# A hybrid decoder layer on one Trainium2 core: u and y of the state-space layer re-laid through DRAM instead of by TensorE transposes, with a new spread of the filler products and a new split of the first feed-forward products

## The chip, the core and the metric

The kernel runs on one core of one Trainium2 chip. The metric is the device time of one execution in microseconds (us); the time of a kernel is the median of its runs.

## The reference

One layer of a decoder with 1024 tokens and a model width of 1024, all in float32. Three token mixers read column blocks of one projection of the normed input, their outputs are gated and summed, and a SwiGLU feed-forward follows:

```
h = rms_norm(x, mix_norm_g)
(u, c_b, c_c, c_x, q, k_c, v_c, ..., nsa_gates, mix_gates) = split(h @ w_in)
y_ssm  = s5_mixer(u, ...)                          # 32 groups of 16 channels, 64 complex states each
y_conv = short_conv_mixer(c_x, c_b, c_c, ...)      # width-3 causal convolution, 512 channels
y_attn = nsa_mixer(q, ...)                         # compressed, selected and window attention, 8 heads
x = x + (g0 * y_ssm + g1 * y_conv + g2 * y_attn) @ w_out
h = rms_norm(x, ffn_norm_g)
x = x + (silu(h @ w_gate) * (h @ w_up)) @ w_down   # hidden width 2816
```

In `s5_mixer` a state runs along the tokens, `s[t] = lam_bar * s[t-1] + b_bar u[t]`; `y = Re(c s) + d * u` goes through GELU, then through a gated linear unit (`ssm_w_glu`).

## The kernel before

**Dense products.** Every large product is made of two-part numbers: `split` writes a rounded high part with ScalarE (L61) and the remainder with VectorE (L62), and `prod` issues three matmuls of 128x512 per 128 rows of depth (L120, L122, L124). Weights come as pages of 128x1024 in the order of `weight_list`. `weights()` hands out the next page; when it does, it splits that page and `LOOK` pages ahead, and issues the loads of `AHEAD` pages beyond the last split one. `LOOK` is 1 and `AHEAD` 2 in the stages spoken of here. Working tiles of 128x1024 share 44 buffers ("pages"), tiles of 128x512 share 14; PSUM is divided into four tiles of 128x512 (`acc`) and two of 128x1024 (`wide`).

**Order.** The program is traced once, and a planner makes the order of each engine from it at build time, by the place in the program and by when it reckons the operands to be ready. Each engine and the DMA queue of SyncE (SP) then works in that fixed order. `k.filler` is a generator of dense products; `fill(n)` draws n matmuls from it at that place of the program. In the state-space stage the filler is `tail`: the convolution mixer (12 blocks of 48 matmuls) and the two plain gated projections `mix_plain` (8 pages of 48 matmuls), 960 matmuls in all. `drain` draws the rest.

**The state-space stage.** `u_rows` computes u token-major (tokens on partitions), writes it to DRAM and reads it back with eight interleaved token sets beside each other (`UN`, 32 DMAs at L702). Tokens are handled in 128 chunks of 8; channels in 4 quarters q of 8 groups. For each quarter `s5` does:

- `s5_kernel`: the 8-token kernel of a group (16 matmuls L969), spread by 16 DMAs into `M` (L980);
- `s5_order` and `s5_tokens`: ScalarE reorders `UN` into `UG` (L1001), TensorE transposes it (8 matmuls against the identity, L1010), ScalarE copies the result to `UT` (L1011);
- `s5_carry`, `s5_inputs`: `cp` by 4 DMAs (L958), `Bm` by 8 transposes (L991);
- `s5_scan`: 16 matmuls (L1021), then VectorE multiplies and scans along the chunks (L1037 to L1060), with `beat()`, which is `fill(F5B)`, behind each operation; then the tables of the next quarter (L895, L930 to L947), again a beat behind each operation;
- `s5_out`: y of a chunk from `U` and `M` (L1071) and from the carried state `X` and `cp` (L1075), GELU on ScalarE (L1078), 8 transposes (L1084), a ScalarE copy to `yT` (L1085), and the split into parts (`mhi`, `mlo`).

`mix_ssm` then reads the parts of all four quarters, quarter by quarter in each sum.

**Around the feed-forward's start.** `out_rows` ends with the row norms of the last four token tiles; their normed rows `xn` are transposed (L1361) into operands `B` of a Strassen-like product. The generator `ffn_up` is advanced between those steps with `next(up)`: it issues products of 12 matmuls (L1505) until its next `yield`. The yields stand in front of products 3, 6, 9 and 12 (counted from 0).

Of the kernel before, what the change touches and what calls it, by code (L numbers as in the profile page):

```python
# [8 lines left out]
F32 = mybir.dt.float32  # L9
F32R = mybir.dt.float32r  # L10
# [5 lines left out]
P = 128  # L16
# [17 lines left out]
class Trunk:  # L34
# [639 lines left out]
                yield from self.block(w, (self.hh, self.hl), range(KD), evac)  # L674


    def u_rows(self):
        nc = self.nc
        W = [self.weights() for _ in range(4)]
        self.UN = [self.page("UN") for _ in range(4)]  # L680
        self.tab = {}

        def ahead():
            yield from self.s5_phases()
            yield from self.s5_tables(0, self.tab)
        steps = ahead()
        spill = self.dram.tile([S, HALF], F32, tag="su", name="su")
        for t in range(NT):
            ps = self.acc()
            tok = slice(t * P, (t + 1) * P)  # L690
            yield from self.prod(ps, (lambda k: self.hh[k][:, tok], lambda k: self.hl[k][:, tok]),
                                 (lambda k: W[k // 2][0][:, (k % 2) * 512:(k % 2) * 512 + 512],
                                  lambda k: W[k // 2][1][:, (k % 2) * 512:(k % 2) * 512 + 512]), range(KD))
            u = self.half("u")
            nc.scalar.activation(u, ps, AF.Copy)
            nc.sync.dma_start(spill[tok], u)
            for _ in range(8):
                next(steps, None)
        chunk = spill.rearrange("(n j) c -> j n c", j=8)
        for q in range(4):  # L700
            for k in range(8):
                nc.sync.dma_start(self.UN[q][:, k * P:(k + 1) * P], chunk[7 - k][:, q * P:(q + 1) * P])  # L702
        self.run(steps)


    def conv_rows(self):
        nc = self.nc
        self.cv, self.gp, self.gn_at = [], {}, 0
        for c in range(4):
            if c == 3:  # L710
                self.gate_fetch(0)
                self.gate_fetch(1)
            cb, cy, cv = self.page("cb"), self.page("cy"), self.page("cv")
            z = self.page("z")

            def evac_c(half, s, ps):
                nc.scalar.activation(cb[:, s], ps, AF.Copy)

            def evac_x(half, s, ps):
                nc.vector.tensor_tensor(z[:, s], ps, cb[:, s], op=OP.mult)  # L720
                if half == 0:
                    return
                w = [self.par[:, R_CW + k * 4 + c:R_CW + k * 4 + c + 1] for k in range(3)]
                nc.vector.tensor_scalar(cy, z, w[2], None, op0=OP.mult)
                nc.vector.scalar_tensor_tensor(cy[:, 1:], z[:, :1023], w[1], cy[:, 1:], op0=OP.mult, op1=OP.add)
                nc.vector.scalar_tensor_tensor(cy[:, 2:], z[:, :1022], w[0], cy[:, 2:], op0=OP.mult, op1=OP.add)

            def evac_b(half, s, ps):
                nc.vector.tensor_tensor(cv[:, s], ps, cy[:, s], op=OP.mult)
            for evac in (evac_c, evac_x, evac_b):  # L730
                yield from self.block(self.weights(), (self.hh, self.hl), range(KD), evac)
            self.cv.append(self.halves(cv))


    def cmul(self, eng, o, a, b, t, conj=False):
# [259 lines left out]
        self.fill(2 * self.F5)  # L995
        return B

    def s5_order(self, q):

        self.ug[q] = self.page("UG")  # L1000
        self.nc.scalar.activation(self.ug[q].rearrange("p (g k h) -> p g k h", g=8, k=8),  # L1001
                                  self.UN[q].rearrange("p (k g h) -> p g k h", k=8, g=8), AF.Copy)

    def s5_tokens(self, q):
        nc = self.nc
        U = self.page("UT").rearrange("p (g n) -> p g n", g=8)
        un = self.ug.pop(q)
        ps = self.wide()
        for g in range(8):
            nc.tensor.transpose(ps[:, g * P:(g + 1) * P], un[:, g * P:(g + 1) * P], self.ident)  # L1010
        nc.scalar.activation(U.rearrange("p g n -> p (g n)"), ps, AF.Copy)  # L1011
        self.fill(2 * self.F5)
        return U

    def s5_scan(self, q, U, B, ep):
        nc = self.nc
        v = nc.vector
# [44 lines left out]
        return X  # L1062

    def s5_out(self, q, U, M, X, cp):
        nc = self.nc
        Y = self.page("YN").rearrange("p (t g h) -> p t g h", t=8, g=8)
        ps = self.wide()
        for half in range(2):
            b = ps[:, half * 512:half * 512 + 512]
            for j in range(4):  # L1070
                nc.tensor.matmul(b[:, j * P:(j + 1) * P], U[:, half * 4 + j], M[:, half * 2 + j // 2, j % 2],  # L1071
                                 start=j == 0, stop=False, skip_group_check=True)
            for j in range(4):
                a, g = half * 2 + j // 2, j % 2
                nc.tensor.matmul(b[:, j * P:(j + 1) * P], X[:, a, g], cp[:, a, g], start=False, stop=j == 3,  # L1075
                                 skip_group_check=True)
            self.fill(self.F5)
        nc.scalar.activation(Y.rearrange("p t g h -> p g t h"), ps.rearrange("p (g t h) -> p g t h", g=8, t=8),  # L1078
                             AF.Gelu_apprx_tanh)
        self.fill(self.F5)  # L1080
        yT = self.page("yT")
        ps = self.wide()
        for t in range(8):
            nc.tensor.transpose(ps[:, t * P:(t + 1) * P], Y[:, t].rearrange("p g h -> p (g h)"), self.ident)  # L1084
        nc.scalar.activation(yT.rearrange("p (n t) -> p t n", t=8), ps.rearrange("p (t n) -> p t n", t=8), AF.Copy)  # L1085
        self.fill(self.F5)
        self.yT.append(self.halves(yT))

    F5, F5S = 8, 16
    F5B = 3  # L1090

    def beat(self):

        self.fill(self.F5B)

    def s5(self):
        self.yT, self.ug = [], {}
        tab = self.tab
        for q in range(4):
            bp, cr, bb, ep = tab.pop(q)  # L1100
            M = self.s5_kernel(q, cr, bb)
            if q == 0:
                self.s5_order(0)
            cp = self.s5_carry(cr)
            U = self.s5_tokens(q)
            B = self.s5_inputs(q, bp)
            if q < 3:
                self.s5_order(q + 1)
            self.F5B = 3 if q < 3 else 5
            X = self.s5_scan(q, U, B, ep)  # L1110
            if q < 3:
                for _ in self.s5_tables(q + 1, tab):
                    self.beat()
            self.fill(self.F5S)
            self.s5_out(q, U, M, X, cp)


    def halves(self, x):
# [274 lines left out]
    def ffn_up(self):  # L1393
# [84 lines left out]
            operand(n)  # L1478
        yield
        for n, (i, z, p) in enumerate(flat):  # L1480
            if n in (3, 6, 9, 12):
                yield
            if n == len(flat) - 5:
                self.down = self.ffn_down()
# [145 lines left out]
    def weight_list(self):  # L1630
        i = self.i
        w = i["w_in"][0]
        ks = [self.cols(w, 4 * a, 4, C_KS, 256) for a in range(2)]
        kw = [self.cols(w, 3 * b, min(3, KD - 3 * b), C_KW, 280) for b in range(3)]
        L = [ks[0], kw[0], ks[1], kw[1], kw[2]]
        L += [self.cols(w, 0, KD, C_KC, P), self.cols(w, 0, KD, C_VC, P)]
        L += [self.cols(w, 2 * a, 2, C_Q, 512) for a in range(4)]
        w1 = [self.cols(i["cmp_w1"][0, n // 4], 4 * (n % 4), 4, 0, 256, "w1") for n in range(8)]
        g = [self.cols(w, 0, KD, C_MG + n * P, P, "g") for n in range(24)]
        L += g[:2] + w1[:3] + g[2:3] + w1[3:7] + g[3:4] + w1[7:] + g[4:]  # L1640
        L += [self.cols(w, 2 * a, 2, C_U, 512) for a in range(4)]
        for c in range(4):
            L += [self.cols(w, 0, KD, c0 + c * P, P) for c0 in (C_C, C_X, C_B)]
        for m in (i["conv_w_out"][0], i["nsa_w_o"][0]):
            L += [self.cols(m, 0, 4, d * 256, 256) for d in range(4)]
        gl = i["ssm_w_glu"][0]

        def glu(d):
            def f(t):
                v = t.rearrange("p (z k c) -> p z k c", z=2, k=4)  # L1650
                return [(v[:, z], gl[:, z * D + d * P:z * D + d * P + P].rearrange("(k p) c -> p k c", p=P))
                        for z in range(2)]
            f.used, f.key = 1024, None
            return f
        L += [glu(d) for d in range(KD)]
        return L
# [3 lines left out]
def trunk_kernel(ctx, tc, ins, out):  # L1660
# [61 lines left out]
        k.fill(n or 1)  # L1722
    k.attention()
    k.drain()
    k.run(k.u_rows())

    def tail():
        yield from k.conv_rows()
# [7 lines left out]
                o.append(k.halves(raw[d - 4]))  # L1736
        yield from k.mix_plain(1, k.cv, True, split)
        yield from k.mix_plain(2, o, False)
    k.filler = tail()
    k.fill(24)  # L1740
    k.s5()
    k.drain()
    k.run(k.mix_ssm())
    k.out_rows()
    k.run(k.down)
# [23 lines left out]
```

## Time and profile before

| what | value |
|---|---|
| median of 3 runs (lowest to highest) | 1762.75 us (1761.01 to 1764.09) |
| the profiled execution: its time, its span | 1763.58 us, 1761.7 us |
| mean granted TensorE clock over the span | 0.999 |
| TensorE matmul busy | 1738.1 us (99% of the span), 8701 matmuls |
| VectorE, ScalarE, GpSimd busy | 1198.2 us (68%), 793.7 us (45%), 83.7 us (5%) |
| DMA queue of SyncE | 184.08 MB, 32.5% of the 16 engines' time |

The span is the time from the first to the last instruction of the profiled execution; 1.9 us of that execution lie outside it. TensorE's busy time counts a matmul from its start to its modelled end, which overlaps the next one, so the engine's rate is read from the starts of successive matmuls.

### The profile page before, as it was taken

The numbers are of one execution on the slowest core, as the hardware profiler recorded it, in microseconds if no ns is written. First come the engines' busy times: TensorE is split into PE (matmuls) and PEld (weight loads), VectorE is DVE, ScalarE is ACT, GpSimd is POOL, SyncE is SP. The second block draws the span as 40 slices with busy tenths as digits, with TensorE's granted clock in tenths as the row PEclk, the third lists the DMA queues.
The fourth block names the chain that finished last, engine by engine and source line by source line (L and its number), as shares of the span: only waits on it lengthen the run. The fifth ranks groups of instructions, "written<-read, shape, count | busy, mean of one in ns | idle before, by whom it ended". The sixth has DMA issues, their size and how long they took to land.

```text
span 1761.7 us, 23773 instructions
## 1 busy us (share of the span) xinstructions
PE 1738.1 (99%) x8701; PEld 1440.4 (82%) x8701; DVE 1198.2 (68%) x2434; ACT 793.7 (45%) x1469; POOL 83.7 (5%) x86
## 2 busy tenths in 40 slices
PE   8999999999999999999999999999999999999999
PEld 7987788888888888888888888778888888888887
DVE  6975456666666670856875687698667776697681
ACT  6415567777777842222132234742223233344360
POOL 0000000000000000000000000002112111110000
PEclk9999999999999999999999999999999999999999
DMA  5213422221211123322554323433222322477521
GB/s 171 73 43 103 122 84 67 60 61 45 60 41 49 55 83 91 83 60 73 179 175 137 108 96 102 144 120 127 101 96 102 120 96 90 169 272 252 163 95 48
DMA packets 166202, 185.60 MB, mean 105 GB/s; under 512 B 17642, under 2 KB 122182, under 8 KB 166086
## 3 DMA queue, kind: packets, MB, share of 16 engines
q1 hardware_dynamic: 166053, 184.08, 32.5%
q8 instruction: 69, 1.13, 0.3%
q14 instruction: 48, 0.39, 0.1%
q10 hardware_dynamic: 32, 0.01, 0.0%
HBM read 132.40 MB, written 45.35 MB: 101 GB/s over the span
## 4 chain that ended last, share of the span: by engine, by line
PE 82%; DVE 9%; ACT 4%; issue 2%; SPq 1%; DMA 1%; DVEq 0%; ACTq 0%; POOL 0%
PE wide L1505 12%; PE acc L124 11%; PE acc L120 11%; PE acc L122 11%; PE acc L1612 7%; PE acc L1505 7%; PE wide L1612 5%; PE acc L560 3%; PE wide L519 3%; PE acc L1274 2%; PE wide L1274 2%; DVE A L62 2%; PE acc L582 2%; PE acc L583 2%; PE wide L257 1%
## 5 line engine op out<-in xcount | busy, mean ns | idle before, releaser
L1505 PE MATMUL wide<-B,A 128*128 128x512 f32 x1056 | 250.8, 391 | 0.6 <-ACT A L61 0.3
L120 PE MATMUL acc<-hh,whi 128*128 128x512 f32 x608 | 243.4, 400 | 2.8 <-DVE kl L66 1.5
L124 PE MATMUL acc<-hh,wlo 128*128 128x512 f32 x608 | 243.0, 400 | 1.4 <-DVE wlo L62 1.4
L122 PE MATMUL acc<-hl,whi 128*128 128x512 f32 x608 | 243.1, 400 | 0.0
L1505 PEld LDWEIGHTS wide<-B,A 128*128 128x128 f32 x1056 | 196.6, 188 | 47.5 <-DVE sg L1518 3.3
L1505 PE MATMUL acc<-B,A 128*128 128x512 f32 x792 | 192.1, 393 | 0.5 <-ACT p L1508 0.5
L1505 PEld LDWEIGHTS acc<-B,A 128*128 128x128 f32 x792 | 149.2, 189 | 32.6 <-ACT p L1508 1.6
L62 DVE TENSOR_TENSOR wlo<-raw,whi 128x1024 fp32r<-128x1024 f32 (+1 forms) x75 | 90.6, 1211 | 72.4 <-ACT whi L61 56.0
L120 PEld LDWEIGHTS acc<-hh,whi 128*128 128x128 f32 x608 | 114.6, 188 | 21.0 <-issue 2.0
L124 PEld LDWEIGHTS acc<-hh,wlo 128*128 128x128 f32 x608 | 114.8, 189 | 18.8 <-DVE wlo L62 2.1
L61 ACT ACTIVATE A<-S 128x512 fp32r<-128x512 f32 x88 | 55.0, 627 | 166.8 <-DVE S L1437 166.0
L122 PEld LDWEIGHTS acc<-hl,whi 128*128 128x128 f32 x608 | 114.6, 189 | 17.3 <-issue 0.2
L62 DVE TENSOR_TENSOR ptl<-acc,pth 128x512 fp32r<-128x512 f32 (+1 forms) x152 | 93.8, 619 | 48.6 <-ACT pth L61 47.4
L1612 PE MATMUL acc<-wdp,act 128*128 128x512 f32 x528 | 121.2, 389 | 0.0
L524 DVE CUSTOM_DVE_ANT_0 p<-wide,mask 128x640 f32<-128x640 f32 (+7 forms) x128 | 90.1, 705 | 43.2 <-PE wide L519 40.5
L1612 PEld LDWEIGHTS acc<-wdp,act 128*128 128x128 f32 x528 | 99.1, 188 | 20.6
L527 ACT ACTIVATE p<-p,small 128x640 f32<-128x640 f32 (+7 forms) x128 | 93.6, 732 | 37.0 <-DVE small L524 34.9
L61 ACT ACTIVATE pth<-acc 128x512 fp32r<-128x512 f32 (+1 forms) x152 | 80.9, 534 | 45.2 <-PE acc L560 44.4
L61 ACT ACTIVATE whi<-raw 128x1024 fp32r<-128x1024 f32 (+1 forms) x75 | 77.6, 1045 | 52.2 <-DVE m L1154 15.9
L120 PE MATMUL acc<-mhi,whi 128*128 128x512 f32 x256 | 100.1, 392 | 0.3 <-DVE m L1154 0.3
L1461 POOL TENSOR_TENSOR sg<-sg 128x512 f32<-128x512 f32 x44 | 72.2, 1642 | 590.3 <-DVE sg L1450 361.9
L122 PE MATMUL acc<-mlo,whi 128*128 128x512 f32 x256 | 99.9, 390 | 0.2 <-DVE mlo L62 0.2
(402 smaller groups left out, 3369.2 us busy)
## 6 DMA issues: line engine op xcount, KB each, us to landing
raw<-in_ffn_w_gate_up_dram SPq DMA_DIRECT2D x52, 512.0 KB, 4.6
raw<-in_w_in_dram SPq DMA_DIRECT2D x48, 512.0 KB, 4.3
sa<-sg SPq DMA_DIRECT2D x77, 256.0 KB, 2.0
araw<-sa SPq DMA_DIRECT2D x77, 256.0 KB, 3.5
sg<-tg SPq DMA_DIRECT2D x48, 256.0 KB, 2.2
gp<-sg SPq DMA_DIRECT2D x24, 512.0 KB, 5.7
x<-in_x_dram SPq DMA_DIRECT2D x16, 512.0 KB, 4.6
wd<-in_ffn_w_down_dram SPq DMA_DIRECT2D x11, 512.0 KB, 6.8
```

The source lines that it names most:

```text
L61: self.nc.scalar.activation(hi, src, AF.Copy)
L62: self.nc.vector.tensor_tensor(lo, src, hi.bitcast(F32), op=OP.subtract)
L120: self.nc.tensor.matmul(out, hi(k), mh(k), start=start and j == 0, stop=False)
L122: self.nc.tensor.matmul(out, hi(k), ml(k), start=False, stop=False)
L124: self.nc.tensor.matmul(out, lo(k), mh(k), start=False, stop=stop and j == n - 1)
L519: nc.tensor.matmul(ps[:, c * 512:c * 512 + w], self.QS[t][:, h], k[:, k0 + c * w:k0 + c * w + w], start=z == 0, stop=z == 1)
L524: nc.vector.tensor_tensor_reduce(p[:, :n].rearrange("p (c w) -> p c w", c=pieces), v, m.rearrange("p (c w) -> p c w", c=pieces), scale=-1. ...
L527: nc.scalar.activation(p[:, :n], p[:, :n], AF.Exp, scale=-1.0, bias=st[:, hh:hh + 1], accum_out=st[:, 2 + hh:3 + hh])
L1274: nc.tensor.matmul(ps, act[:, x * 512 + t * P:x * 512 + (t + 1) * P], w[:, y * 512:y * 512 + 512], start=i == 0 and j == 0 and p in (1, 5, ...
L1461: e.tensor_tensor(o, x, y, op=op)
L1505: nc.tensor.matmul(ps, x, y, start=p in (1, 5, 6, 7) and k + j == 0, stop=k == 3 and j == 2, skip_group_check=True)
L1612: nc.tensor.matmul(ps, act[:, x * 512 + t * P:x * 512 + (t + 1) * P], w[:, y * 512:y * 512 + 512], start=i == 0 and j == 0 and p in (1, 5, ...
```

## The change

- u is computed channel-major (`u_blocks`): each quarter is one weight page and one `block`, whose two halves ScalarE writes to a page `ut` (8 tokens of a chunk apart). The page goes to DRAM and comes back by 8 DMAs as `U`, with token-in-chunk and channel on partitions: the layout that `UT` had. `s5_order`, `s5_tokens` and their transposes go.
- In `s5_out` the operands of the matmuls change places, so that y comes out with token-in-chunk and channel on partitions. GELU writes it to a page, one DMA writes that to DRAM, and 8 DMAs read it back channel-major as `yT`. The transposes L1084 and the copy L1085 go.
- The split of y into parts is a step of its own, `s5_parts`, and reads `yT` with a stride of 128 elements. It stands behind `s5_inputs` of the next quarter; for the last quarter behind 32 more filler matmuls.
- A beat is 3.5 matmuls on the average instead of 3 in the first three quarters (5 in the last, as before); the fills of `s5_tokens` and one of `s5_out` go.
- The split of a convolution quarter into parts moves behind the first block of the next quarter.
- `LOOK` is 2 from the start of the filler to the end of `drain`.
- In `ffn_up` the yields stand in front of products 5, 7, 9 and 12.

```diff
-    def u_rows(self):
+    def u_blocks(self):
...
         for q in range(4):
+            ut = self.page("ut").rearrange("p (j n) -> p j n", j=8)
+            def evac(half, s, ps):
+                nc.scalar.activation(ut[:, :, half * 64:half * 64 + 64], ps.rearrange("p (n j) -> p j n", j=8), AF.Copy)
+                for _ in range(8):
+                    next(steps, None)
+            yield from self.block(self.weights(), (self.hh, self.hl), range(KD), evac)
+            spill = self.dram.tile([P, 8, P], F32, tag=f"su{q}", name=f"su{q}")
+            nc.sync.dma_start(spill, ut)
+            U = self.page("UT").rearrange("p (g n) -> p g n", g=8)
+            back = spill.rearrange("(g h) j n -> j h g n", g=8)
             for k in range(8):
-                nc.sync.dma_start(self.UN[q][:, k * P:(k + 1) * P], chunk[7 - k][:, q * P:(q + 1) * P])
+                nc.sync.dma_start(U[k * 16:(k + 1) * 16], back[7 - k])
+            self.U.append(U)
...
     def conv_rows(self):
...
-            self.cv.append(self.halves(cv))
+                if evac is evac_c and last is not None:
+                    self.cv.append(self.halves(last))
+            last = cv
+        self.cv.append(self.halves(last))
...
     def s5_out(self, q, U, M, X, cp):
...
-                nc.tensor.matmul(b[:, j * P:(j + 1) * P], U[:, half * 4 + j], M[:, half * 2 + j // 2, j % 2],
+                nc.tensor.matmul(b[:, j * P:(j + 1) * P], M[:, half * 2 + j // 2, j % 2], U[:, half * 4 + j],
...
-                nc.tensor.matmul(b[:, j * P:(j + 1) * P], X[:, a, g], cp[:, a, g], start=False, stop=j == 3,
+                nc.tensor.matmul(b[:, j * P:(j + 1) * P], cp[:, a, g], X[:, a, g], start=False, stop=j == 3,
...
+        nc.scalar.activation(Y, ps, AF.Gelu_apprx_tanh)
+        spill = self.dram.tile([P, 8, P], F32, tag=f"sy{q}", name=f"sy{q}")
+        nc.sync.dma_start(spill, Y.rearrange("p (g n) -> p g n", g=8))
+        yT = self.page("yT").rearrange("p (t n) -> p t n", t=8)
+        back = spill.rearrange("(t h) g n -> g h t n", t=8)
+        for g in range(8):
+            nc.sync.dma_start(yT[g * 16:(g + 1) * 16], back[g])
+        self.fill(2 * self.F5)
+        self.last = yT
+
+    def s5_parts(self):
+        hi, lo = self.page("mhi", F32R), self.page("mlo", F32R)
+        cut = lambda x: x.rearrange("p (n t) -> p n t", t=8)
+        self.split(cut(hi), cut(lo), self.last.rearrange("p t n -> p n t"))
+        self.yT.append((hi, lo))
...
-    F5B = 3
+    F5B, due = 3.5, 0.0
...
     def s5(self):
...
-            U = self.s5_tokens(q)
+            U = self.U[q]
             B = self.s5_inputs(q, bp)
-            if q < 3:
-                self.s5_order(q + 1)
-            self.F5B = 3 if q < 3 else 5
+            if q:
+                self.s5_parts()
+            self.F5B = 3.5 if q < 3 else 5
...
             self.s5_out(q, U, M, X, cp)
+        self.fill(32)
+        self.s5_parts()
...
-            if n in (3, 6, 9, 12):
+            if n in (5, 7, 9, 12):
                 yield
...
-        L += [self.cols(w, 2 * a, 2, C_U, 512) for a in range(4)]
+        L += [self.cols(w, 0, KD, C_U + q * P, P) for q in range(4)]
...
+    k.LOOK = 2
     k.filler = tail()
     k.fill(24)
     k.s5()
     k.drain()
+    k.LOOK = 1
```

## Rows read from the trace of the kernel before

**Rows 1.** The page: busy time of engines, and the granted TensorE clock in slices.
```profile
PE 1738.1 (99%) x8701; PEld 1440.4 (82%) x8701; DVE 1198.2 (68%) x2434; ACT 793.7 (45%) x1469; POOL 83.7 (5%) x86
...
PEclk9999999999999999999999999999999999999999
```
**Rows 2.** Windows: length, busy (count) of PE, PEld, DVE, ACT, POOL; clock, DMA share, GB/s.
```profile
683.00:948.00 265.00, 261.34 (x1317) 218.87 (x1316) 177.31 (x279) 70.48 (x79) 5.83 (x22) 1.00 0.40 118
...
900.00:931.00 31.00, 31.00 (x156) 26.33 (x156) 29.09 (x43) 4.68 (x6) 0.11 (x1) 1.00 0.66 217
```
**Rows 3.** The chain that ended last: start us, us, what (24 matmuls in a row).
```profile
1190.65 5.44 PE acc L1505 x24
```
**Rows 4.** Timeline of TensorE around one transpose group: start us, us, engine, line.
```profile
756.51 0.39 PE L120 MATMUL acc<-hh,whi 128*128 128x512 f32 x1
756.75 1.03 PE L1010 MATMUL wide<-ident,UG 128*128 128x128 f32 x8
757.53 0.48 PE L122 MATMUL acc<-hl,whi 128*128 128x512 f32 x1
757.85 0.40 PE L124 MATMUL acc<-hh,wlo 128*128 128x512 f32 x1
```
**Rows 5.** Timeline of TensorE: its waits in the state-space stage, in brackets.
```profile
734.48 0.50 PE L120 MATMUL acc<-hh,whi 128*128 128x512 f32 x1 [1.24 <-ACT whi L61]
...
801.31 0.50 PE L124 MATMUL acc<-hh,wlo 128*128 128x512 f32 x1 [1.36 <-DVE wlo L62]
...
848.01 0.50 PE L122 MATMUL acc<-mlo,whi 128*128 128x512 f32 x1 [0.21 <-DVE mlo L62]
...
855.83 0.46 PE L1075 MATMUL wide<-cp,X 128*128 128x128 f32 x2 [0.51 <-issue]
856.59 0.47 PE L120 MATMUL acc<-mhi,whi 128*128 128x512 f32 x1 [0.30 <-DVE m L1154]
```
**Rows 6.** Timeline of ScalarE ahead of the first of these waits.
```profile
732.42 1.06 ACT L61 ACTIVATE mhi<-cv 128x1024 fp32r<-128x1024 f32 x1 [19.26 <-DVE cv L729]
733.39 1.04 ACT L61 ACTIVATE whi<-raw 128x1024 fp32r<-128x1024 f32 x1
```
**Rows 7.** Timeline of the SyncE queue: issues, merged by line.
```profile
683.17 0.32 SPq L696 DMA_DIRECT2D su<-u  x1
685.32 15.61 SPq L702 DMA_DIRECT2D UN<-su  x32
...
741.17 0.37 SPq L83 DMA_DIRECT2D raw<-in_w_in_dram  x1
759.34 10.26 SPq L980 DMA_DIRECT2D M<-kz  x16
...
772.44 15.45 SPq L83 DMA_DIRECT2D raw<-in_w_in_dram  x3
```
**Rows 8.** DMA issues: KB each, median us from issue to landing.
```profile
cp<-cr SPq DMA_DIRECT2D x16, 128.0 KB, 2.4
...
sx<-x SPq DMA_DIRECT2D x8, 512.0 KB, 3.7
```
**Rows 9.** Timeline of ScalarE and VectorE at the stage's end.
```profile
930.59 1.03 ACT L1078 ACTIVATE YN<-wide 128x1024 f32<-128x1024 f32 x1 [22.95 <-PE wide L1075]
935.11 2.17 ACT L1085 ACTIVATE yT<-wide 128x1024 f32<-128x1024 f32 x1 [3.49 <-PE wide L1084]
...
939.91 1.22 DVE L62 TENSOR_TENSOR mlo<-yT,mhi 128x1024 fp32r<-128x1024 f32 x1
```
**Rows 10.** Timeline of TensorE, then VectorE, at the feed-forward's start.
```profile
1126.37 0.44 PE L1361 MATMUL wide<-ident,xn 128*128 128x128 f32 x2 [1.92 <-DVE xn L215]
1126.56 5.05 PE L1505 MATMUL acc<-B,A 128*128 128x512 f32 x14
...
1126.23 1.29 DVE L62 TENSOR_TENSOR A<-raw,A 128x512 fp32r<-128x512 f32 x2
```
**Rows 11.** Windows at the feed-forward's start, columns as in the windows above.
```profile
1128.00:1130.00 2.00, 2.00 (x7) 1.54 (x5) 1.35 (x3) 1.31 (x3) 0.00 (x0) 0.50 0.00 0
```

More of the change, by code (lines that the diff above doesn't have):

```diff
@@ L674, in gates @@
                 yield from self.block(w, (self.hh, self.hl), range(KD), evac)
-    def u_rows(self):
+    def u_blocks(self):
         nc = self.nc
-        W = [self.weights() for _ in range(4)]
-        self.UN = [self.page("UN") for _ in range(4)]
-        self.tab = {}
+        self.tab, self.U = {}, []
         def ahead():
@@ L686, in u_rows @@
         steps = ahead()
[L687 to L699, printed above, removed]
-        for q in range(4):
+        for q in range(4):
+            ut = self.page("ut").rearrange("p (j n) -> p j n", j=8)
[8 more added lines that the diff above has]
+            back = spill.rearrange("(g h) j n -> j h g n", g=8)
             for k in range(8):
-                nc.sync.dma_start(self.UN[q][:, k * P:(k + 1) * P], chunk[7 - k][:, q * P:(q + 1) * P])
+                nc.sync.dma_start(U[k * 16:(k + 1) * 16], back[7 - k])
+            self.U.append(U)
         self.run(steps)
@@ L707, in conv_rows @@
         nc = self.nc
-        self.cv, self.gp, self.gn_at = [], {}, 0
+        self.cv, self.gp, self.gn_at, last = [], {}, 0, None
         for c in range(4):
@@ L996, in s5_inputs @@
         return B
[L998 to L1013, printed above, removed]
     def s5_scan(self, q, U, B, ep):
@@ L1065, in s5_out @@
         nc = self.nc
-        Y = self.page("YN").rearrange("p (t g h) -> p t g h", t=8, g=8)
+        Y = self.page("YN")
         ps = self.wide()
@@ L1074, in s5_out @@
                 a, g = half * 2 + j // 2, j % 2
-                nc.tensor.matmul(b[:, j * P:(j + 1) * P], X[:, a, g], cp[:, a, g], start=False, stop=j == 3,
+                nc.tensor.matmul(b[:, j * P:(j + 1) * P], cp[:, a, g], X[:, a, g], start=False, stop=j == 3,
                                  skip_group_check=True)
             self.fill(self.F5)
[L1078 to L1087, printed above, removed]
+        nc.scalar.activation(Y, ps, AF.Gelu_apprx_tanh)
[12 more added lines that the diff above has]
+        self.yT.append((hi, lo))
     F5, F5S = 8, 16
-    F5B = 3
+    F5B, due = 3.5, 0.0
     def beat(self):
-        self.fill(self.F5B)
+        self.due += self.F5B
+        self.fill(int(self.due))
+        self.due -= int(self.due)
     def s5(self):
-        self.yT, self.ug = [], {}
+        self.yT = []
         tab = self.tab
@@ L1101, in s5 @@
             M = self.s5_kernel(q, cr, bb)
-            if q == 0:
-                self.s5_order(0)
             cp = self.s5_carry(cr)
-            U = self.s5_tokens(q)
+            U = self.U[q]
             B = self.s5_inputs(q, bp)
-            if q < 3:
-                self.s5_order(q + 1)
-            self.F5B = 3 if q < 3 else 5
+            if q:
+                self.s5_parts()
+            self.F5B = 3.5 if q < 3 else 5
             X = self.s5_scan(q, U, B, ep)
@@ L1724, in trunk_kernel @@
     k.drain()
-    k.run(k.u_rows())
+    k.run(k.u_blocks())
     def tail():
```

## The prediction, made before the changed kernel was run

> **What bounds the kernel now.** I read the page first. TensorE is busy for 99% of the span and its granted clock is full in all 40 slices [rows 1], so time can only go where matmuls go or where TensorE waits. Busy time overlaps, so I take its rate from starts: 24 matmuls of 128x512 in a row take 5.44 us [rows 3], 0.227 us each. Next, the windows of the state-space stage with its filler, 683 to 948 us: VectorE is busy 177.31 of 265 us there, ScalarE 70.48 [rows 2]. TensorE bounds the stage as a whole. VectorE bounds stretches of it: in the last scan, 900 to 931 us, it is busy 29.09 of 31 us [rows 2]. Last, the timelines: TensorE's own waits in the stage are five, with 1.24 + 1.36 + 0.21 + 0.51 + 0.30 = 3.62 us in brackets [rows 5].
>
> The profiled execution took 1763.58 us (span 1761.7 and 1.88 around it), 0.83 us over the median of the runs. I make the sum against it and take 0.8 off at the end.
>
> **Transposes removed.** Eight transposes stand between two dense matmuls: the dense one at 756.51 us is followed, over the group and one more dense one, by the next at 757.85 [rows 4]. That is 1.34 us for the group and two dense matmuls of 0.227, so a group costs 0.89 us. There are eight groups (L1010 and L1084, one each per quarter): 8 x 0.89 = **-7.1 us**. As TensorE is the bound, this goes straight off the span; the end at which it gives nothing is a rival below. The swapped operands of `s5_out` and the u blocks keep number and shape of their matmuls: 0. The ScalarE copies that go (per quarter about 1.06, 1.03 and, for `yT`, 2.17 us [rows 9]) lie under TensorE's work: 0. With them gone a bank of `wide` is free sooner, a gain that I put at 0.
>
> **Waits in the stage.** The first, 1.24 us, is for a weight's high part. On ScalarE that split stood behind `mhi<-cv`, the split of a finished convolution quarter, which had waited 19.26 us for VectorE [rows 6]. The second, 1.36 us, is for a weight's remainder on VectorE [rows 5]. `LOOK` 2 places each weight split one block of 48 matmuls, 10.9 us, earlier, and the convolution's split now stands a block later; both delays are short against 10.9 us. What is late next is the 0.21 wait for a convolution's remainder, and the 0.81 us around `s5_out`, which I leave. So **-2.6 us**; bounds 0 (other waits take their place) and -3.6. A beat of 3.5 puts 0.11 us more of TensorE's work beside each VectorE operation; the fills add up to nearly the same: by the code 885 matmuls were drawn when `s5_out` of the last quarter begins, and 885.5 are now. No cost, no gain.
>
> **The u stage.** Its weights come as one page per quarter instead of four for all; U of the first quarter starts on its way after the first of four blocks, three blocks (33 us) ahead of the stage, where `UN` kept SP until 700.9 us [rows 7]. TensorE does not wait there before, so 0; if U were late, 24 + 8 + 16 filler matmuls, 10.9 us, stand ahead of its use.
>
> **The new trip of y.** For each quarter one DMA of 512 KB goes out, SP waits for its landing, and eight DMAs of 64 KB come back. The landing of 512 KB in DRAM takes 3.7 us [rows 8]. An issue of a strided DMA costs SP 10.26 / 16 = 0.64 us at `M`, 15.61 / 32 = 0.49 at `UN` [rows 7]; I take 0.62 for these, nearest to `M` (16 partitions), so eight take 5.0. The last lands 2.4 us after its issue (`cp` [rows 8]). The split into parts took from 938.04 to 941.1 on both engines (from `yT`, 2.17 us, on to the end of `mlo` at 939.91 + 1.22 [rows 9]); its two pieces are about 1.05 and 1.22 us. In the first three quarters this trip has the next quarter's kernel, inputs and scan beside it, over 40 us: 0. In the last it stands on the way to `mix_ssm`. From the end of `s5_out`'s matmuls, 930.6 us: GELU to 931.6 [rows 9], write landed 935.4, eight reads issued by 940.4, landed 942.8, high part 943.9, remainder 945.1. That is 13.3 us for the high part and 14.5 us for the remainder, counted from 930.6. Ahead of `mix_ssm` are 74.5 - 8 = 66.5 filler matmuls, 15.1 us, and its first sum takes nine matmuls of the other quarters, 2.0 us, before it needs the last one. So there are 17.1 us of cover for 13.3 to 14.5 us of trip. The margin is under 4 us on a DMA system that is busy for 0.66 of that time [rows 2]; I charge **+0.5 us**, with bounds 0 and +5 (three late, and a slow stretch of the clock as below).
>
> The row for `yT` bears on the split's stride: the copy that wrote with a stride of 8 elements took 2.17 us where the GELU of the same 128x1024 took 1.03 [rows 9]. The Trainium skill, SBUF — State Buffer, "Door 1: The DMA port swizzle", says that access beyond a 16-byte line costs extra, 4 float32 being the free stride; the split now reads at 128. The row agrees with the rule for a write. By it each piece of the split would double, the trip of the last y would become about 17 us, the cover would be just used up, and the other quarters would lose nothing.
>
> **SP's queue.** In each of the first three quarters the trip adds to SP about 3.7 + 5.0 = 8.7 us in which nothing else is issued; queued behind are the 16 issues for `M`, four for `cp` and the weight pages. Before, no weight page was issued from 741.2 to 772.4 us [rows 7], 31 us, against a cover of three pages (one split ahead, two loaded), 3 x 10.9 = 32.7. Now about 40 us stand against four pages, 43.6. No cost, but it is the closest thing to one.
>
> **The feed-forward's start.** TensorE waits 1.92 us for the last normed row, and the 14 matmuls behind the wait take 5.05 us [rows 10], where 14 x 0.227 and the last one's overlap of 0.16 are 3.34: 1.7 us lost at a granted clock of 0.50, the 1.2 GHz level [rows 11], after an idle stretch. Five products ahead of the transposes could cover the wait, -3.6 us. But products 3 and 4 need their operands, which VectorE made from 1126.23 us [rows 10], no earlier than the row for which TensorE waited. Nothing in the change brings them forward, so I take **-0.5**; bounds -3.6 and +3.6 (a second such wait, as the transposes come two products, 5.4 us, later).
>
> **Sum.** -7.1 - 2.6 + 0.5 - 0.5 = -9.7: 1753.9 us for an execution like the profiled one, 1753.1 for the median. I predict **1753 us**.
>
> **Rivals.**
> - *The trip of the last y sets the end.* If the last y comes 3 us late, TensorE waits 3 us, and a wait of 1.9 us was enough for 1.7 us at half clock [rows 10, 11]. Then 1753 + 5 = 1758 us. For it: the short margin, and the doubling that the strided write shows [rows 9]. Against: four quarters in each sum, three of them there, and four `acc` banks, so the planner can start further sums.
> - *VectorE takes the time over.* Where it is full (29.09 of 31 us [rows 2]) TensorE gains nothing from fewer matmuls, and the order runs at VectorE's pace; the transposes' 7.1 us become waits, and the two mended waits return: about 1762 us. Against: VectorE is busy only two thirds of the stage.
> - *SP falls behind: slower.* If the 44 page buffers are all held, the fourth weight page cannot be loaded ahead and the cover stays 32.7 us against 40: TensorE waits 7 us in each of three quarters, and the following matmuls run at half clock for 1.7: 3 x 9 = 27 us, 1780 us. The point from which it decides is a gap between weight issues of more than 43.6 us, or of 32.7 if the extra page is not granted. For it: a weight load issued at 772.44 us took SP 15.45 us for three [rows 7], so pages are short already. Against: U, back early, replaces `UN`, `UG` and `UT`, which frees two pages.
>
> **How the numbers follow.** A median moved by less than 0.2%, 3.5 us, I count as the same. Chances: forecast 0.56, late last y 0.13, VectorE 0.17, SP 0.14. Of the forecast's own range, 1746 to 1758, the low end is both bounds that gain (-3.6 at the feed-forward, -3.6 in the stage and no charge for y: 1763.6 - 14.3 - 0.8 = 1748.5) with 2 us for banks freed sooner; the high end has both at no gain and half the late y. The range 1746 to 1764 adds late y and VectorE, and leaves out SP and some of the edges. Faster by over 0.2% (under 1759.2): the forecast, and most of late y, 0.69. Within 0.2%: most of VectorE and some of late y, 0.17. Slower: SP, 0.14.
>
> **What would show it.** Right: no L1010 and no transposes on `YN`; 8637 matmuls; the stage some 9 us shorter; no wait over 1 us for `whi` or `wlo` between 683 and 940 us. The last y: the split's end less the GELU's start below 16 us, and no wait of TensorE on `mhi` or `mlo`. Wrong: TensorE waits on `whi` behind a raw load whose SP issue stands behind the reads of y (SP); on `X`, `cb` or `z` with VectorE full (VectorE); a longer loss between the last out products and the first `wide` product of the feed-forward.

## The result and the profile after

The changed kernel takes 1774.61 us (median of 4 runs, 1772.42 to 1775.03), the kernel before 1763.12 on the same chip: a ratio of 1.0064, interval [1.0049, 1.0079]. It is 11.5 us slower; 1753 was predicted. The profiled span grows by 10.8 us, from 1761.7 to 1772.5.

The page of the changed kernel, against [rows 1]: the 64 transposes are gone, and a slice of the granted clock is no longer full.

```profile
PE 1736.4 (98%) x8637; PEld 1436.3 (81%) x8637; DVE 1200.7 (68%) x2434; ACT 782.1 (44%) x1457; POOL 87.5 (5%) x86
...
PEclk9999999999999999999899999999999999999999
```

The windows of the changed kernel, columns as in [rows 2]: the stage, and then inside it.

```profile
683.00:948.00 265.00, 249.14 (x1203) 206.57 (x1202) 171.37 (x272) 55.05 (x64) 7.95 (x22) 0.97 0.38 114
...
770.00:780.00 10.00, 10.00 (x46) 8.29 (x45) 0.00 (x0) 0.00 (x0) 0.00 (x0) 1.00 0.52 137
...
840.00:850.00 10.00, 5.50 (x37) 4.83 (x35) 5.26 (x6) 1.19 (x2) 0.00 (x0) 1.00 0.85 266
850.00:860.00 10.00, 7.67 (x24) 5.86 (x25) 9.97 (x20) 3.06 (x3) 0.00 (x0) 0.66 0.56 212
860.00:870.00 10.00, 6.80 (x20) 5.11 (x19) 9.79 (x16) 0.00 (x0) 0.00 (x0) 0.70 0.30 105
```

In the same 265 us TensorE gets through 1203 matmuls where it was 1317 [rows 2], 64 of these the transposes. VectorE does nothing at all from 770 to 780 us and is full from 850 to 870. It is not short of time on the average; its work comes bunched. In the changed kernel it waits most for V, the scan's input, which TensorE makes from `U` and `Bm`. Its waits in front of the copy of V from 683 to 948 us (total us, times, longest), first in the kernel before, then in the changed one:

```profile
DVE V L1030 <- PE wide L1021: 14.9, 3, 6.9
DVE V L1014 <- PE wide L1005: 55.2, 4, 25.9
```

TensorE's waits of the changed kernel from 683 to 948 us, grouped (total us, times, longest), against the five of [rows 5]:

```profile
PE acc L120 <- DVE cv L727: 9.1, 3, 6.8
PE wide L1060 <- issue: 5.4, 3, 3.2
PE acc L120 <- ACT cb L715: 1.1, 1, 1.1
PE wide L1060 <- DVE X L1044: 0.2, 1, 0.2
```

Neither `whi` nor `wlo` is in the list: the waits that the change was reckoned to mend are mended. In their place stand other waits: 15.8 us in all against 3.6, +12.2. Most are for an `acc` bank that VectorE has not emptied (`cv`), and for the carried state. The view calls the latter "issue", but the timeline of VectorE has an operation that writes `X` (L1044) from 864.16 to 864.84 us, and TensorE starts on `X` at 864.94.

The longest one in the timelines, TensorE first and then VectorE (start us, us, engine, line; idle time before it in brackets):

```profile
842.43 0.39 PE L124 MATMUL acc<-mhi,wlo 128*128 128x512 f32 x1
842.66 1.95 PE L1005 MATMUL wide<-UT,Bm 128*128 128x128 f32 x16
844.44 1.06 PE L1056 MATMUL wide<-UT,M 128*128 128x128 f32 x8
852.33 0.80 PE L120 MATMUL acc<-mhi,whi 128*128 128x512 f32 x1 [6.83 <-DVE cv L727]
852.92 0.63 PE L122 MATMUL acc<-mlo,whi 128*128 128x512 f32 x1
853.35 0.63 PE L124 MATMUL acc<-mhi,wlo 128*128 128x512 f32 x1
...
857.24 0.39 PE L120 MATMUL acc<-mhi,whi 128*128 128x512 f32 x1
...
864.94 0.77 PE L1060 MATMUL wide<-X,cp 128*128 128x128 f32 x2 [3.20 <-issue]
```

```profile
827.67 1.29 DVE L718 TENSOR_TENSOR z<-acc,cb 128x512 f32<-128x512 f32 x2 [3.29 <-PE acc L122]
836.84 2.06 DVE L62 TENSOR_TENSOR mlo<-yT,mhi 128x1024 fp32r<-128x1024 f32 x1 [7.88 <-ACT mhi L61]
844.64 0.68 DVE L1014 COPY V<-wide 64x512 f32<-64x512 f32 x1 [5.74 <-PE wide L1005]
845.25 0.73 DVE L722 TENSOR_SCALAR cy<-z,par 128x1024 f32<-128x1024 f32 x1
...
851.59 0.68 DVE L727 TENSOR_TENSOR cv<-acc,cy 128x512 f32<-128x512 f32 x1
...
855.85 1.21 DVE L62 TENSOR_TENSOR mlo<-cv,mhi 128x1024 fp32r<-128x1024 f32 x1
...
864.16 0.68 DVE L1044 TENSOR_TENSOR X<-m,m 64x508 f32<-64x508 f32 x1
```

VectorE works in a fixed order, and the copy of V stands in it ahead of the convolution (`cy`, `cv`). The convolution's input `z` is done at 828.96 us, but V's matmuls (L1005) come from TensorE only at 842.66. VectorE waits 5.74 us for them with the convolution queued behind V; then both come at once, TensorE finds no empty bank, waits 6.83 us, and starts its next matmuls 0.43 us apart instead of 0.227. The windows show the clock: 0.50 from 852 to 857 us and again from 865 to 870, the 1.2 GHz level:

```profile
852.00:857.00 5.00, 4.67 (x11) 3.41 (x12) 5.00 (x11) 2.99 (x3) 0.00 (x0) 0.50 0.73 286
865.00:870.00 5.00, 5.00 (x12) 3.89 (x13) 4.90 (x8) 0.00 (x0) 0.00 (x0) 0.50 0.11 43
```

Eleven starts take 4.91 us behind the first wait (852.33 to 857.24) and twelve take 5.22 behind the second (865.62 to 870.84); at 0.227 that would be 2.5 and 2.7, so 4.9 us are lost to the clock.

The account: -7.1 (transposes, as the prediction reckoned them) + 12.2 (waits) + 4.9 (clock) = +10.0 of the +10.8 us.

### The profile page after: what moved, and what is told of

The parts are those of the page before. It is cut to its first block, busy times and chain, and to the rows that moved or that the text cites. A ratio compares the mean times of both kernels' runs of the same rounds, so it can differ in the third digit from the quotient of the medians.

```text
span 1772.5 us, 23670 instructions
## 1 busy us (share of the span) xinstructions
PE 1736.4 (98%) x8637; PEld 1436.3 (81%) x8637; DVE 1200.7 (68%) x2434; ACT 782.1 (44%) x1457; POOL 87.5 (5%) x86
## 4 chain that ended last, share of the span: by engine, by line
PE 81%; DVE 11%; ACT 4%; issue 2%; DMA 1%; POOL 0%; SPq 0%; POOLq 0%; ACTq 0%; DVEq 0%
PE wide L1497 11%; PE acc L120 11%; PE acc L122 11%; PE acc L124 11%; PE acc L1497 6%; PE acc L1604 5%; PE wide L1604 5%; PE acc L560 3%; PE wide L519 3%; PE acc L1266 2%; DVE A L62 2%; PE wide L1266 2%; PE acc L583 2%; PE acc L582 2%; DVE S L1429 1%
## 5 line engine op out<-in xcount | busy, mean ns | idle before, releaser
L120 PE MATMUL acc<-hh,whi 128*128 128x512 f32 x672 | 269.1, 401 | 5.0 <-DVE cv L727 2.3
L122 PE MATMUL acc<-hl,whi 128*128 128x512 f32 x672 | 267.9, 399 | 0.0
L124 PE MATMUL acc<-hh,wlo 128*128 128x512 f32 x672 | 267.0, 398 | 0.0
L120 PEld LDWEIGHTS acc<-hh,whi 128*128 128x128 f32 x672 | 126.6, 188 | 26.4 <-ACT cb L715 4.1
L124 PEld LDWEIGHTS acc<-hh,wlo 128*128 128x128 f32 x672 | 126.8, 189 | 19.9 <-DVE wlo L62 0.4
L122 PEld LDWEIGHTS acc<-hl,whi 128*128 128x128 f32 x672 | 126.6, 188 | 19.5 <-issue 0.2
```

The costliest lines, as they stand in the source:

```text
L120: self.nc.tensor.matmul(out, hi(k), mh(k), start=start and j == 0, stop=False)
L122: self.nc.tensor.matmul(out, hi(k), ml(k), start=False, stop=False)
L124: self.nc.tensor.matmul(out, lo(k), mh(k), start=False, stop=stop and j == n - 1)
```

## The experiments

Two theories stood against each other. **V late**: TensorE's built order places the scan-input matmuls too far behind the transposes for `Bm`, as above. **VectorE overloaded**: the strided split and the beats of 3.5 give VectorE more than fits. Beside them stood the trips through DRAM (SP) and the feed-forward's yields. In each run the time of before is that of the same chip.

**1. LOOK at 1** in the changed kernel.

```diff
-    k.LOOK = 2
+    k.LOOK = 1
```

> The changed kernel with LOOK left at 1. Theory 'V late' (the order puts the scan-input matmuls of a quarter too many dense matmuls behind the transposes for Bm; VectorE stands idle in front of the copy of V, with the convolution's evacuations queued behind it, and is full afterwards, so TensorE waits for acc banks and X): dense matmuls between the two fall from 106, 114, 85, 40 to 72, 66, 67, 40; TensorE's waits of 9.1, 5.4 and 1.1 us fall to about a third; 1762 to 1767 us. Theory 'VectorE overloaded' (strided split and beats of 3.5): same work on VectorE, so 1773 to 1776 us.

1766.01 us, ratio 1.0021 [1.0011, 1.0031], some 8 us less than with LOOK 2. Its waits in the stage are 8.4 us:

```profile
PE acc L124 <- DVE wlo L62: 6.2, 3, 4.1
PE wide L1060 <- issue: 1.9, 2, 1.5
PE acc L120 <- DVE m L1146: 0.3, 1, 0.3
```

VectorE's idle time in front of V falls from 55.2 to 36.2 us. The waits for `wlo` are back, 6.2 us against 1.4 before the change: with VectorE bunched this remainder is late too. VectorE's busy time is the same (1201.5 us against 1200.7), so overload alone is out.

**2. LOOK 2 alone**, in the kernel before (the same line, the other way).

> The kernel before with LOOK 2 in the state-space stage and nothing else. 'V late': 50, 64, 66, 29 dense matmuls between Bm's transposes and the scan's input, where it was 29, 48, 37, 29; 1765 to 1770 us, with a wait for acc banks of 2 to 5 us. As the prediction had it (the two waits for whi and wlo mended): 1760 to 1761 us.

1764.37 us, 1.0009 [1.0000, 1.0019]: no gain of 2.6 us; the small loss is not clear of noise. The time lies between the two ranges expected. The waits of TensorE in its stage:

```profile
PE acc L120 <- DVE m L1154: 4.4, 4, 2.8
PE acc L120 <- DVE cv L729: 1.3, 1, 1.3
```

Those for `whi` and `wlo` are gone, as the prediction had it, and 5.7 us of waits for banks stand in their place.

**3. u and y alone**: the changed kernel with LOOK 1, beats of 3, and the convolution's split and the yields of before.

```diff
-    F5B, due = 3.5, 0.0
+    F5B, due = 3, 0.0
...
-            if n in (5, 7, 9, 12):
+            if n in (3, 6, 9, 12):
...
-    k.LOOK = 2
+    k.LOOK = 1
```

> The changed kernel with only u and y re-laid: LOOK 1, beats of 3, the convolution's split and the feed-forward's yields as before. 'V late': 72, 87, 84, 97 dense matmuls, so part of the loss stays: the transposes' -7.1 us against waits of 5 to 10: 1761 to 1768 us. If the trips through DRAM themselves cost (SP, pages): about 1772 to 1775 us. If the re-laying is clean and the rest of the change is the loss: 1756 us.

1767.60 us, 1.0028 [1.0019, 1.0038]. The re-laying alone makes the kernel slower although 64 transposes go. Beats of 3.5, the convolution's split and the yields, which run 1 has on top, don't carry the loss: run 1 is 1.6 us lower, with intervals that overlap.

**4. V first**: the changed kernel, LOOK 2 and all, with the order of `s5` turned (`s5_v` holds the matmuls and copies of V, taken out of `s5_scan`; the split of y, `s5_parts`, now stands behind V too).

```diff
+            U = self.U[q]
+            B = self.s5_inputs(q, bp)
+            V = self.s5_v(U, B)
             M = self.s5_kernel(q, cr, bb)
             cp = self.s5_carry(cr)
-            U = self.U[q]
-            B = self.s5_inputs(q, bp)
```

> The changed kernel, LOOK 2 and all, but the scan's input (Bm, V) stands in front of the 8-token kernel K of each quarter. Dense matmuls between Bm's transposes and the scan-input matmuls: 46, 14, 16, 13 in place of 106, 114, 85, 40. 'V late': VectorE's idle stretches in front of V go, TensorE's waits for acc banks and X fall under 4 us together: 1755 to 1763 us. 'VectorE overloaded': the work on VectorE is the same, so 1772 to 1776 us.

1754.61 us, 0.9954 [0.9939, 0.9969], just under the range expected: some 19 us less than the changed kernel (0.0110 between the ratios), with the same instructions on every engine. The trips through DRAM stand in it as before, so they don't carry the loss. (The order that was built has 46, 18, 16 and 19 dense matmuls between the two; the expectation miscounts two of them.) One group of waits is left in the stage:

```profile
PE wide L1061 <- DMA M<-kz: 2.7, 2, 2.5
```

**5. V first in the kernel before**, transposes kept (there `s5_tokens`, `s5_inputs`, `s5_v` ahead of `s5_kernel`).

> The kernel before (transposes and all) with the scan's input in front of the 8-token kernel, as in the run before: 8, 16, 16, 16 dense matmuls between Bm's transposes and the scan-input matmuls instead of 29, 48, 37, 29. 'V late' with the transposes at 7.1 us on TensorE's path: V was hardly late before, so at most its waits in the stage go (2 to 4 us): 1759 to 1763 us, some 5 to 8 us above the changed kernel with the same order (1754.6). Rival, that the order of V is worth about 8 us to any version and the re-laying nothing: 1754 to 1756 us.

1756.85 us, 0.9965 [0.9952, 0.9978], and TensorE has no wait in the stage. It lies between the two ranges expected: the order is worth more to the kernel before than was thought, and less than to the changed one. The profiled spans differ by 6.6 us. Of these 3.6 are the waits of [rows 5], all of them gone, those for `whi` and `wlo` too; 1.7 are the half clock at the feed-forward's start [rows 10, 11], which this execution doesn't have; 1.3 are not accounted for.

**6. V first with LOOK 1**, the line of run 1 on top of run 4.

> The changed kernel with V first and LOOK 1. If LOOK 2 harms only by making V late: within 2 us of the same with LOOK 2 (1754.6), 1753 to 1757 us. If LOOK 2 costs by itself (pages, splits on VectorE): 1749 to 1752 us. If it is needed for the waits on whi and wlo, as the prediction had it: 1757 to 1760 us, with such waits of 2.6 us in the stage.

1751.27 us, 0.9933 [0.9917, 0.9950]: with run 7 the fastest kernel, 11.8 us below before. Its waits in the stage, and the stage's window:

```profile
PE wide L1061 <- DMA M<-kz: 0.7, 1, 0.7
```

```profile
683.00:948.00 265.00, 264.24 (x1304) 221.73 (x1303) 186.04 (x283) 58.45 (x67) 7.90 (x18) 1.00 0.45 138
```

In 265 us 1304 matmuls now, none of them a transpose of u or y, and 186 us of VectorE's work instead of 171: the engine that looked overloaded does more in the same time. No wait for `whi` or `wlo` came back, so LOOK 2 isn't needed. The time lies in the range that was expected if LOOK 2 costs by itself, but runs 4 and 6 are not clear of each other (their intervals overlap), and run 4 waits 2.0 us more for `M`. The remaining 5.6 us between runs 5 and 6 hold the transposes' gain and the smaller edits.

**7. The 8-token kernel right behind V's matmuls**, LOOK 2: V's own fill moves behind `s5_carry`.

```diff
-        self.fill(2 * self.F5)
         return V
...
             cp = self.s5_carry(cr)
+            self.fill(2 * self.F5)
```

> The changed kernel, V first, and the 8-token kernel directly behind V's matmuls (no filler between). The wait of 2.5 us for M in the third quarter of V first alone is shorter if the kernel's matmuls come earlier: they stand right at V's in all quarters; 1751 to 1754 us. If the wait for M is from the DMAs on SP and not from the matmuls' place: 1754 to 1756 us.

1751.94 us, 0.9939 [0.9924, 0.9954]. The third quarter's wait of 2.5 us for `M` is gone: SP issues its DMAs from 824.16 us on, in run 4 from 829.43. So the place of the kernel's matmuls made it. One wait is left:

```profile
PE wide L1060 <- issue: 0.8, 1, 0.8
```

In this kernel L1060 is the matmul of `U` and `M`, in the fourth quarter. SP issues the DMAs for `M` there until 894.30 us, and TensorE starts at 895.18: a wait for `M` again, whatever the view calls it. LOOK is 2 here and the time that of run 6, so LOOK 2 by itself costs nothing that these runs can tell.

**8. Both mends together**: run 7 with LOOK 1.

> The changed kernel with LOOK 1, V first, and the 8-token kernel directly behind V's matmuls: both mends together. If they are for different waits (banks and M): 1748.5 to 1750.5 us; if they mend the same wait: 1751 to 1752 us.

1760.97 us, 0.9989 [0.9980, 0.9998]: a miss. The waits:

```profile
PE wide L1060 <- DMA M<-kz: 6.5, 1, 6.5
PE wide L1060 <- issue: 0.7, 1, 0.7
```

The order that is built for this mix has TensorE ready for the first matmuls on `M` at 709.2 us, while SP issues the DMAs for `M` only from 704.68 on, 10.18 us long. In run 7 these matmuls stand at 718.52. The two mends together made another order, and their gains don't add.

**9. V late again**: run 6 with 48 more matmuls between `Bm` and V, taken from the fills behind.

```diff
-        self.fill(2 * self.F5)
+        self.fill(8 * self.F5)
         return B
...
-        self.fill(2 * self.F5)
         return V
...
-        self.fill(2 * self.F5)
         self.last = yT
...
-            self.fill(self.F5S)
             self.s5_out(q, U, M, X, cp)
```

> V first with LOOK 1 (1751.3 us), made late on purpose: 48 more filler matmuls between Bm's transposes and the scan's input, taken from the fills behind it, so that the number of fills is the same. Dense matmuls between the two: 70, 64, 64, 47 instead of 46, 17, 16, 19. 'V late': VectorE's idle time in front of V grows from 30 to over 50 us, and TensorE waits for acc banks, z, cv or X: 1756 to 1764 us. Rival, that V first gains by something else (the kernel's matmuls or M's DMAs at another place): 1750 to 1753 us.

1762.89 us, 0.9998 [0.9989, 1.0008]: 11.6 us lost again, from fillers moved alone. The waits:

```profile
PE acc L124 <- DVE wlo L62: 3.9, 2, 3.3
PE wide L1060 <- DMA M<-kz: 3.0, 2, 2.0
```

Three things in the expectation failed. VectorE's idle time in front of V is 20.3 us, not over 50, and is lower than in run 6 (29.8, of which 18.4 are the first quarter's and cost TensorE nothing). So that idle time doesn't rank kernels; what counts is what is queued behind V and who needs it. The waits are for `wlo`, not for banks, `z`, `cv` or `X`; the longest, 3.3 us, falls in the fourth quarter, where VectorE doesn't stand idle in front of V at all but is nearly full from 896.5 to 922 us. And 3.0 of the 6.9 us are for `M`, which this edit delays too. So the run shows that moved fillers alone can cost what V first gained; that all of it comes through V it does not show.

**10 and 11. u alone and y alone** re-laid, in the kernel before (the diff's `u_blocks` without its `s5_out` and `s5_parts`, and the reverse).

> The kernel before with u alone re-laid (four groups of transposes less, 3.6 us). Dense matmuls between Bm's transposes and the scan's input 72, 69, 62, 38 instead of 29, 48, 37, 29. 'V late': VectorE's idle time in front of V 25 to 35 us (13 before), and new waits of TensorE eat the 3.6: 1761 to 1766 us. If only the transposes count: 1759 us.

> The kernel before with y alone re-laid (the other four groups of transposes less, 3.6 us). Dense matmuls between Bm's transposes and the scan's input 29, 55, 62, 29. 'V late': somewhat late in the third quarter alone, 1758 to 1762 us. If y's trip (SP, the strided split) costs TensorE time: 1763 us and more, with waits on mhi, mlo or on weights behind SP.

u alone: 1767.60 us, 1.0027 [1.0017, 1.0036], above the range expected, with 8.9 us of waits in the stage. y alone: 1760.38 us, 0.9986 [0.9977, 0.9995], with 4.4. Each takes 32 transposes away; y's re-laying leaves V nearly where it was (V is awaited 11.3 us in all; 14.9 before) and keeps most of its gain. u's makes VectorE wait 32.5 us and loses more than it saves.

**12. The yields alone**, in the kernel before.

> The kernel before with the feed-forward's yields of the changed kernel alone (in front of products 5, 7, 9, 12). The prediction's term: -0.5 us, bounds -3.6 and +3.6. The changed kernel's trace shows the same wait of 1.9 us for xn and the slow clock behind it, so 1761.5 to 1763.5 us, not to be told from before.

1762.90 us, 1.0000 [0.9990, 1.0009]: nothing.

## Why the prediction was wrong

**Transposes, -7.1: right as far as shown.** There are 8637 matmuls, and 5.6 us lie between the two kernels with V first, beside smaller edits. Of the profiled executions run 6 alone has a wait in the stage, 0.7 us, and the half clock at the feed-forward's start, 1.7 us (0.75, 0.50 and 0.90 from 1114 to 1120); with these the spans, 1755.1 and 1749.9, come to 7.6 us apart.

**Waits in the stage, -2.6 with bounds 0 and -3.6: this step failed.** The mechanism that it named holds: LOOK 2 does end the waits for `whi` and `wlo` (the changed kernel, and run 2). But it took the two waits as delays by themselves and the rest of the order as fixed. The whole order is made anew: with LOOK 2 and with U there early (runs 1, 2 and 10 take them one by one), the scan's input moved from 29, 48, 37, 29 dense matmuls behind `Bm`'s transposes to 106, 114, 85, 40. The term measured +12.2 us of waits and 4.9 of half clock. Its upper bound, 0, left out that a mended wait can return larger at another tile. **The u stage, 0,** failed in the same way: U was early as reckoned, but u alone costs 4.6 us where its 32 transposes were to give 3.6 (run 10). **The beat, 0,** rested on the same assumption, that counts of fills tell where matmuls end up; its own effect was not measured.

**VectorE takes the time over, 1762 us: right in kind, too small in price.** Of the waits that the prediction named for it, those for `X` (5.6 us) and `cb` (1.1) came; the largest, 9.1 us for banks behind `cv`, it did not name, and the waits for `whi` and `wlo`, which it had return, did not. It was priced as a gain that vanishes, with an average load of two thirds against it; a bunched VectorE also adds waits, and the average says nothing about that.

**The last y, +0.5: nothing, within its bounds; its trip was mis-sized.** The timelines of ScalarE and VectorE in the changed kernel, against [rows 9]:

```profile
941.09 1.03 ACT L1063 ACTIVATE YN<-wide 128x1024 f32<-128x1024 f32 x1 [18.11 <-PE wide L1060]
950.89 2.11 ACT L61 ACTIVATE mhi<-yT 128x1024 fp32r<-128x1024 f32 x1 [7.83 <-DMA yT<-sy]
...
958.11 2.02 DVE L62 TENSOR_TENSOR mlo<-yT,mhi 128x1024 fp32r<-128x1024 f32 x1
```

From the GELU's start to the remainder's end it takes 19.0 us, not 14.5: each piece takes 2.0 to 2.1 us, and the remainder starts 5.1 us behind the high part's end (953.0 us), after other work of VectorE. TensorE waits for neither part all the same, so the margin was larger than reckoned. The strided read costs nearly what the prediction weighed: 2.06 us for `mlo<-yT` against 1.21 for `mlo<-cv` in the timeline above. The Trainium skill, SBUF — State Buffer, "Door 1: The DMA port swizzle", says that access beyond a 16-byte line costs extra; by this trace that holds for a read too.

**SP: right, nothing.** The queue of the changed kernel, against [rows 7]:

```profile
704.84 40.89 SPq L83 DMA_DIRECT2D raw<-in_w_in_dram  x5
...
750.60 3.64 SPq L1069 DMA_DIRECT2D yT<-sy  x8
```

Five loads are drawn out over 40.9 us, and TensorE waits for no weight in the changed kernel's stage. The eight reads of y take 3.64 us, not 5.0.

**The feed-forward, -0.5: nothing** (run 12), as its bounds had it; the wait is the same as in [rows 10]:

```profile
1135.92 0.44 PE L1353 MATMUL wide<-ident,xn 128*128 128x128 f32 x2 [1.92 <-DVE xn L215]
1136.12 5.05 PE L1497 MATMUL acc<-B,A 128*128 128x512 f32 x14
```

**Left open:** why the planner places V later when u's transposes go or when LOOK is 2 (no trace shows its reckoning); 1.3 us of run 5's gain; and the beat and the convolution's split each by itself, which were not tried.

## What to carry to other kernels

Where a planner makes one order per engine, an edit that adds slack is not a local edit: find the step that the in-order engine must pass first (here the copy of V) and ask where its input lands in the other engine's new order, before pricing the waits that go. An engine busy for two thirds can still set the pace where it idles in front of one instruction and has the rest queued behind it. Putting the producer of that instruction first was worth 6 us here in the kernel before, about as much as all the transposes, and some 19 in the changed one.

## What was not expected of the hardware

The clock does not fall behind every wait. In the changed kernel it was granted at 0.50 behind waits of 6.83 and 3.20 us. At the feed-forward's start a wait of 1.92 us was enough in the kernel before [rows 10, 11], but behind 1.91 us at the same place in run 5 (up to 1121.30 us) the windows from 1120 to 1128 us show 1.00. In run 2 it is 1.00 too behind 2.83 us (from 852.2 to 855.01 us; the window from 854 to 858). That is one execution: of the ten of run 2, three, the shortest (1762.82 to 1763.73 us), have a mean granted clock of 1.000 over the span and seven (1764.16 to 1765.83 us) of 0.998. So the same order meets the lower level in some executions and not in others, and what a wait costs in clock can't be read from one trace. What tells these apart the traces here don't show.
